# Earlier weights for the last two down-projection units, wider modulation columns, and low parts last in two first blocks

## The chip, the cores and the metric

The kernel runs on one core of one Trainium2 chip. The metric is the device time in microseconds (us) of one execution; three executions of the kernel before gave 900.03 to 900.54 us.

## The reference

One batch of 256 tokens of width 1024 passes two transformer blocks in float32. What matters here is the end of the first and the start of the second:

```python
# first block, end
h = rms_norm(x, ln_ffn_pre)
f = (silu(h @ w_ffn_gate) * (h @ w_ffn_up)) @ w_ffn_down     # hidden width 2816
x = x + rms_norm(f, ln_ffn_post)
# second block, start
mod = silu(c) @ w_ada + b_ada                                # six rows of 1024
sh1, sc1, g1, sh2, sc2, g2 = split(mod, 6)
u = rmsnorm(h, norm_mix_g) * (1 + sc1) + sh1
z = u @ w_in                                                 # 4296 columns
```

Before these stand the two attentions and the mixing of the first block, after them the retention, the sparse attention, and 16 experts of which each token takes two.

## The kernel before, in words

**Products in three.** Every float32 operand of a large product is split in a high part, which ScalarE writes (line 302), and a low part, raw less high, which VectorE writes (line 304). A product is then three matmuls per 128 rows of k (`mm3`, lines 320 to 322): high by high, activation high by weight low, activation low by weight high. Tokens stand in two chunks of 128, c = 0 and c = 1. The activation is the stationary operand, the weight the moving one.

**Weights.** `stream` requests a piece of weights on SP's queue into one of three raw buffers; `unit` splits it into one of four `hi` and four `lo` buffers, or, for `units_ahead`, into tiles of the large pool, so that a block's weights can lie split before its activation exists. A raw buffer is free again when its low parts are written. SP's queue is in order: a request that waits for a raw buffer holds those behind it.

**Order.** A scheduler places the instructions of each engine by their order in the program and by what is ready in its own model. `after(ins)` puts an instruction behind another one of the same engine. In the `with tc.manual_schedule` block near the end of `build` TensorE's order is the program's.

**The first join** is at the start of the first block's feed-forward: `post_norm` of chunk 0, `raw_T` (transposes, high parts by ScalarE on line 401, low parts by VectorE on line 404), then the gate's first 512 columns from units split ahead (`ready`), with chunk 1's norm and transposes between the two chunks' products.

**The second join** is between the blocks. The down-projection runs by units of 256 hidden rows (`out_step`, 11 units, numbers 0 to 10), the last two in one step: all of chunk 0 first, then, behind `mod_row(2)`, all of chunk 1. Its sums stand in three `s` banks and one `o` bank of PSUM. For a chunk then come `post_norm` (squares on ScalarE, line 247; a multiply by the gain, line 415; a row of one-column operations for the root, lines 255 to 265 and 422, 423; the update of x, line 428), `row_rstd` (squares and root again), `modulated_T` (two multiplies, line 379; eight transposes, line 361; eight high parts, line 385; eight low parts, line 388) and its products with two blocks of `w_in_2` split ahead, 512 columns (`ready`) and 200 columns (`ready2`). The table `ENGS` says for each norm and chunk whether the root's one-column operations are on VectorE (V) or GpSimd (G). `mod_cols` turns a row of the modulation into columns by eight products with ones (line 589), each of which TensorE takes in two passes; it stands twice, for rows 3 and 4, behind chunk 0's products.

Of the kernel before, what the change touches and what calls it, by code (L numbers as in the profile page):

```python
# [13 lines left out]
ALU = mybir.AluOpType  # L14
# [3 lines left out]
D = 1024  # L18
FF = 2816
EPS = 1e-6  # L20
AHEAD = (1, 2)
ENGS = ("VG", "VV", "VV", "VG", "VV")
ORDER = "0ab1cqkdgKgQ"
RSQRT_MAGIC = 1597463007.0 - 2.0 ** 22 - 2.0 ** 31
GN_EPS = 1e-5
# [88 lines left out]
def build(tc, A, out, dbg=None):  # L114
# [12 lines left out]
    with es:  # L127
# [47 lines left out]
        def P(which, shape):  # L175
            return {"s": ps_s, "o": ps_o, "b": ps_b}[which].tile(shape, F32, tag=which, name=which)
# [63 lines left out]
        def col(name, j=0, n=1):  # L240
            return colp[:, COL[name] + j:COL[name] + j + n]
# [43 lines left out]
        def stream(shape, srcs):  # L285
            raw = rawp.tile(shape, F32, tag="raw", name="raw")
            for dst, src in srcs(raw):
                nc.sync.dma_start(dst, src)
            return raw

        def unit(raw, ahead=False):

            kc, n = raw.shape[1], raw.shape[2]
            if ahead:
                hi, lo = B([128, kc, n], F32R), B([128, kc, n], F32R)
            else:
# [10 lines left out]
        def units_ahead(w, n0, n, src=None):  # L307

            us = []
            m = 2 if n > 256 else 4  # L310
            for k0 in (0, 4):
                raw = stream([128, 4, n], src(k0) if src else lambda r: [(r, wslice(w, k0, 4, n0, n))])
                us += [unit(raw[:, k:k + m, :], True) for k in range(0, 4, m)]
            return [(k, [b[:, k % m, :] for b in us[k // m]]) for k in range(8)]

        def wslice(w, k0, kc, n0, n):
            return w[k0 * 128:(k0 + kc) * 128, n0:n0 + n].rearrange("(c p) n -> p c n", p=128)

        def mm3(o, a, b, start, stop):
            PE.matmul(o, a[0], b[0], start=start, stop=False)  # L320
            PE.matmul(o, a[0], b[1], start=False, stop=False)  # L321
            return PE.matmul(o, a[1], b[0], start=False, stop=stop)  # L322

        def tok_block(act, w, n0, n, kc=8, src=None, between=None, piece=4, first=None, ready=None):

            acc = [P("b", [128, n]) for _ in range(2)]
            parts = []
            if ready is not None:
                parts = [ready]
            for k0 in range(0, kc if ready is None else 0, 4):  # L330
                m = min(4, kc - k0)
                raw = first if first is not None and not k0 else stream([128, m, n], src(k0) if src else lambda r: [
                    (r[:, i:i + piece], wslice(w, k0 + i, min(piece, m), n0, n)) for i in range(0, m, piece)])
                for k1 in range(0, m, 2):
                    ks = range(k1, min(k1 + 2, m))
                    u = unit(raw[:, k1:ks.stop, :])
                    parts.append([(k0 + k, [b[:, k - k1, :] for b in u]) for k in ks])
            if between and first is None and ready is None:
                parts = [sum(parts, [])]
            for part in parts:  # L340
                for c in range(2):
                    if between and c and part is parts[0]:
                        between(last)
                    for k, b in part:
                        last = mm3(acc[c], [a[k][:, c * 128:(c + 1) * 128] for a in act], b, k == 0, k == kc - 1)
            return acc
# [193 lines left out]
        def modc(i):  # L540
            return modT[:, i, :]
# [40 lines left out]
        def mod_cols(v, pt=None):  # L582

            m = mod_m[v]
            own = pt is None
            if own:
                pt = P("b", [128, 8, 32])
            for k in range(8):
                PE.matmul(pt[:, k, :], m[:, k * 128:(k + 1) * 128], one1[:, 0:32], start=True, stop=True)
            if own:  # L590
                V.tensor_tensor(modT[:, v, :], pt[:, :, 0], col("b_ada_2", v * 8, 8), op=ALU.add)

        ada_gen = ada_steps()

# [311 lines left out]
        def out_acc():  # L906
            return [[P("s", [128, 512]), P("s", [128, 512])], [P("s", [128, 512]), P("o", [128, 512])]]

        def out_step(acc, acts, w, j, nk, between=None):

            us = []
            for i in range(len(acts)):
                raw = stream([128, 2, D], lambda r: [(r, wslice(w, 2 * (j + i), 2, 0, D))])
                us.append([unit(raw[:, :, h * 512:(h + 1) * 512]) for h in range(2)])
# [62 lines left out]
        modvars = {}  # L977

        def block2_shift(pm):
            V.tensor_tensor(modT[:, 3:5, :], pm[:, :, :, 0], col("b_ada_2", 24, 16).rearrange("p (a b) -> p a b", a=2),  # L980
                            op=ALU.add)

        def block2_mods():
            pm = P("b", [128, 2, 32])
# [82 lines left out]
        for b in range(1, 6):  # L1067
            acts += turned_acts(ts)
            n = 512 if b < 5 else 256
            ts = hidden_rows(tok_block(hT, w_fg, b * 512, n), b * 512, n)  # L1070
            out_step(oacc, acts[2 * b - 2:2 * b - 1], w_fd, 2 * b - 2, 22)
            if b == 2:
                gain1 = load_row(A["norm_mix_g_2"])
            if b < 5:
                out_step(oacc, acts[2 * b - 1:2 * b], w_fd, 2 * b - 1, 22)
                ada(9)
            else:
                block2_rel()
            if b == 3:
                first_mods()  # L1080
        acts += turned_acts(ts)
        w_in2 = A["w_in_2"][0]
        ready = units_ahead(w_in2, 0, 512)

        ready2 = units_ahead(None, 0, 200, lambda k0: lambda r: [
            (r[:, :, 0:128], wslice(w_in2, k0, 4, 3584, 128)), (r[:, :, 128:200], wslice(w_in2, k0, 4, 4224, 72))])

        dtv = modvars["dtv"]
        cos2 = lambda c: K(f"cos{c}")
# [5 lines left out]
        turns = []  # L1095
        g1s = []

        def products(acc, units, c):
            for k, b in units:
                i = mm3(acc[c], [a[k][:, c * 128:(c + 1) * 128] for a in uT], b, k == 0, k == 7)  # L1100
            return i

        with tc.manual_schedule(engines={mybir.EngineType.PE}):
            out_step(oacc, acts[9:], w_fd, 9, 22, lambda: g1s.append(mod_row(2)))
            post_norm(oacc, post, 0, 2, rfc[0])
            *marks, xni = modulated_T(*uT, 0, row_rstd(0, 4), gain1, modc(0), (), "s")
            accs = [[P("b", [128, n]) for _ in range(2)] for n in (512, 200)]
            products(accs[0], ready, 0)
            products(accs[1], ready2, 0)
            pm = P("s", [128, 2, 8, 32])  # L1110
            mod_cols(3, pm[:, 0])
            mod_cols(4, pm[:, 1])
            post_norm(oacc, post, 1, 2, rfc[1], (), (xni,))
# [606 lines left out]
```

## Time and profile before

| | us |
|---|---|
| median of three runs | 900.38 |
| the profiled execution itself | 899.23 |
| its span, first to last instruction | 897.4 |
| TensorE busy in it | 864.0 (96%) |
| VectorE busy | 646.0 (72%) |
| ScalarE busy | 407.0 (45%) |
| GpSimd busy | 6.3 (1%) |
| mean granted TensorE clock | 0.988 |

Times below are microseconds from the start of the span. The ends of matmuls are modelled, so in a row of matmuls the distance from start to start is read, not the duration. The clock is a share of full speed: 1.00 is 2.4 GHz, 0.50 is 1.2 GHz.

### The profile page before, as it was taken

Reading aid. Unit: us, or ns where it says so; the run is one execution under the profiler, and the core shown is the slowest. Engines: PE = TensorE matmul, PEld = TensorE weight load, DVE = VectorE, ACT = ScalarE, POOL = GpSimd, SP = SyncE. Lnnn points to the kernel's source line nnn. Section 1 sums busy time; section 2 is a strip of 40 time slices with the busy share of each in tenths; the row PEclk is TensorE's granted clock in tenths of the full one; section 3 lists DMA queues with packets and bytes.
Section 4 is the critical chain, followed back from the end, with each engine's and each line's share of the span. In section 5 each row is a group of like instructions: output and inputs, shape, how many; then the busy total and the mean of one; then the engine's idle time right before and its main releaser. Section 6 shows DMA issues by size and latency. Waiting matters only on the chain.

```text
span 897.4 us, 13319 instructions
## 1 busy us (share of the span) xinstructions
PE 864.0 (96%) x4854; PEld 681.4 (76%) x4854; DVE 646.0 (72%) x1579; ACT 407.0 (45%) x737; POOL 6.3 (1%) x20
## 2 busy tenths in 40 slices
PE   8999999999999999999998999999999999999994
PEld 7777877888777788888895788889889987535541
DVE  6788787647986998888876796798865587333424
ACT  6554665556554644443454334433365354211212
POOL 0100000000000000000000000000000001000000
PEclk9999999999999999999998899999999999999998
DMA  8644452528787488988767045556547778699981
GB/s 304 199 159 129 128 166 68 174 83 296 272 298 270 139 285 289 333 313 283 282 204 253 1 141 150 179 159 194 158 133 259 228 252 308 195 384 333 359 324 50
DMA packets 104589, 195.94 MB, mean 218 GB/s; under 512 B 9892, under 2 KB 43547, under 8 KB 104518
## 3 DMA queue, kind: packets, MB, share of 16 engines
q1 hardware_dynamic: 103816, 194.12, 63.4%
q8 instruction: 40, 0.66, 0.3%
q10 hardware_dynamic: 702, 0.91, 0.3%
q14 instruction: 31, 0.25, 0.1%
HBM read 193.94 MB, written 1.06 MB: 217 GB/s over the span
## 4 chain that ended last, share of the span: by engine, by line
PE 76%; DVE 12%; ACT 5%; DMA 3%; issue 2%; POOL 1%; SPq 0%; ACTq 0%; DVEq 0%; POOLq 0%
PE b L322 14%; PE b L321 14%; PE b L320 14%; PE b L1537 6%; DVE lo L304 3%; PE b L1556 3%; PE s L361 3%; PE s L320 3%; PE s L322 3%; PE s L321 3%; ACT hi L302 2%; PE s L462 2%; PE b L1479 2%; PE s L1574 1%; DMA raw<-in_w_in 1%
## 5 line engine op out<-in xcount | busy, mean ns | idle before, releaser
L304 DVE TENSOR_TENSOR lo<-raw,hi 128x512 fp32r<-128x512 f32 (+4 forms) x447 | 270.7, 638 | 89.1 <-ACT hi L302 88.2
L302 ACT ACTIVATE hi<-raw 128x1024 fp32r<-128x1024 f32 (+4 forms) x220 | 218.2, 999 | 232.3 <-PE b L322 103.1
L320 PE MATMUL b<-hi,big 128*128 128x512 f32 (+3 forms) x502 | 190.8, 380 | 1.8 <-ACT hi L302 0.7
L321 PE MATMUL b<-lo,big 128*128 128x512 f32 (+3 forms) x502 | 190.4, 380 | 0.2 <-DVE lo L304 0.2
L322 PE MATMUL b<-hi,big 128*128 128x512 f32 (+3 forms) x502 | 189.7, 378 | 0.0
L321 PE MATMUL b<-big,hi 128*128 128x256 f32 x392 | 112.6, 287 | 0.0
L320 PE MATMUL b<-big,hi 128*128 128x256 f32 x392 | 112.5, 287 | 0.0
L322 PE MATMUL b<-big,lo 128*128 128x256 f32 x392 | 111.3, 284 | 0.0
L320 PEld LDWEIGHTS b<-hi,big 128*128 128x128 f32 x502 | 94.6, 188 | 19.9 <-ACT hi L302 1.5
L321 PEld LDWEIGHTS b<-lo,big 128*128 128x128 f32 x502 | 94.5, 188 | 17.3 <-issue 1.3
L322 PEld LDWEIGHTS b<-hi,big 128*128 128x128 f32 x502 | 94.5, 188 | 17.0 <-issue 0.5
L320 PEld LDWEIGHTS b<-big,hi 128*128 128x128 f32 x392 | 75.2, 192 | 2.2 <-issue 1.7
L321 PEld LDWEIGHTS b<-big,hi 128*128 128x128 f32 x392 | 75.0, 191 | 1.4 <-issue 1.2
L322 PEld LDWEIGHTS b<-big,lo 128*128 128x128 f32 x392 | 75.0, 191 | 0.5 <-issue 0.3
L1537 PE MATMUL b<-big 128*64 128x512 f32 x128 | 57.8, 596 | 0.0
L561 DVE SCALAR_TENSOR_TENSOR big<-big,csil 128x1024 f32<-128x1024 f32 x40 | 51.1, 1278 | 1.2 <-DMA big<-in_w_ada 1.1
L320 PE MATMUL s<-hi,act 128*128 128x512 f32 x66 | 27.1, 410 | 4.5 <-ACT hi L302 4.5
L1556 PE MATMUL b<-big,pT 128*64 128x512 f32 x128 | 28.9, 593 | 1.1 <-DVE pT L1546 1.1
L1537 PE MATMUL b<-raw,big 128*64 128x512 f32 x64 | 28.8, 593 | 0.0
L321 PE MATMUL s<-lo,act 128*128 128x512 f32 x66 | 26.6, 403 | 0.0
L322 PE MATMUL s<-hi,act 128*128 128x512 f32 x66 | 26.4, 400 | 0.0
L1491 ACT ACTIVATE pT<-b 128x256 f32<-128x256 f32 x8 | 3.1, 385 | 49.2 <-PE b L1537 49.2
(373 smaller groups left out, 1316.5 us busy)
## 6 DMA issues: line engine op xcount, KB each, us to landing
raw<-in_w_in SPq DMA_DIRECT2D x34, 1024.0 KB, 5.3
big<-in_w_ada SPq DMA_DIRECT2D x48, 512.0 KB, 6.6
big<-in_w_exp_down SPq DMA_DIRECT2D x32, 512.0 KB, 6.7
raw<-in_w_ffn_down SPq DMA_DIRECT2D x11, 1024.0 KB, 5.0
raw<-in_w_ffn_gate SPq DMA_DIRECT2D x10, 1024.0 KB, 8.0
raw<-in_w_ffn_up SPq DMA_DIRECT2D x10, 1024.0 KB, 5.1
raw<-in_w_o SPq DMA_DIRECT2D x8, 1024.0 KB, 5.7
raw<-in_w_gate SPq DMA_DIRECT2D x8, 1024.0 KB, 5.3
```

The costliest lines, as they stand in the source:

```text
L302: S.activation(hi, raw, AF.Copy)
L304: V.tensor_tensor(lo[:, a:a + m], raw[:, a:a + m], hi[:, a:a + m].bitcast(F32), op=ALU.subtract)
L320: PE.matmul(o, a[0], b[0], start=start, stop=False)
L321: PE.matmul(o, a[0], b[1], start=False, stop=False)
L322: return PE.matmul(o, a[1], b[0], start=False, stop=stop)
L361: turned[:] = [PE.transpose(dst[:, i, :], s, ident)]
L462: PE.matmul(scs[i][:, a:b], q[:, c * 128:(c + 1) * 128], k[:, 0:b - a], start=fresh[i], stop=False)
L561: V.scalar_tensor_tensor(m, wt, csil[:, k:k + 1], m, op0=ALU.mult, op1=ALU.add)
L1479: PE.matmul(pt[:, k, :], xs(c, (2 * k2 + k) * 128, 128), hot[:, c, :], start=(i == 0), stop=(i == 3))
L1537: PE.matmul(pu[i * 64:(i + 1) * 64, :].rearrange("p (a n) -> p a n", a=2), xg[k // 4][:, k % 4, s0:s0 + 64], win[2 * p + i][k], start=(k = ...
L1556: PE.matmul(py[i * 64:(i + 1) * 64, :], hT2[:, k, i * 64:(i + 1) * 64], wdn[2 * p + i][k][:, hs], start=(k == 0), stop=(k == 1))
L1574: PE.matmul(yacc[c][h], hT.bitcast(F32) if one else hT, y, start=False, stop=(p == 7 and (i == 1 or one)))
```

## The change

- The last two down-projection units (9 and 10) are requested and split before the first block of `w_in_2`, where they stood behind it, and behind both halves of the 200-column block.
- The 200-column block is requested in two halves (k 0 to 3 and k 4 to 7). The second is requested behind chunk 1's multiplies in the program, and its low parts are put behind them on VectorE. Chunk 0 is multiplied with the first half early, with the second one late.
- `mod_cols` moves 128 columns of ones in place of 32, at a distance of 16, so that each overwrites most of what the one before wrote and its first column stays. Row 3 comes right behind the down-projection, ahead of chunk 0's transposes; row 4 between chunk 0's two blocks. Their bank is of the `b` pool in place of `s`.
- Both first blocks issue all products of the high activations of a chunk first, then those of the low ones (`chunk_products`).
- In the norm behind the feed-forward (index 2 of `ENGS`) chunk 1's one-column operations go to GpSimd, and its multiplies (line 415) come behind the last low part of chunk 0, where they came behind its line 379.

```diff
-ENGS = ("VG", "VV", "VV", "VG", "VV")
+ENGS = ("VG", "VV", "VG", "VG", "VV")
...
+        def chunk_products(o, act, units, c, start=True, stop=True):
+
+            hi, lo = [[a[k][:, c * 128:(c + 1) * 128] for k, _ in units] for a in act]
+            for i, (k, b) in enumerate(units):
+                PE.matmul(o, hi[i], b[0], start=start and i == 0, stop=False)
+                PE.matmul(o, hi[i], b[1], start=False, stop=False)
+            for i, (k, b) in enumerate(units):
+                last = PE.matmul(o, lo[i], b[0], start=False, stop=stop and i == len(units) - 1)
+            return last
...
# tok_block
+                    if part is ready:
+                        last = chunk_products(acc[c], act, part, c)
+                        continue
...
# mod_cols
-                pt = P("b", [128, 8, 32])
+                pt = P("b", [128, 512])
...
-                PE.matmul(pt[:, k, :], m[:, k * 128:(k + 1) * 128], one1[:, 0:32], start=True, stop=True)
+                PE.matmul(pt[:, k * 16:k * 16 + 128], m[:, k * 128:(k + 1) * 128], one1, start=True, stop=True)
...
-        def out_step(acc, acts, w, j, nk, between=None):
+        def out_units(w, j):
+            raw = stream([128, 2, D], lambda r: [(r, wslice(w, 2 * j, 2, 0, D))])
+            return [unit(raw[:, :, h * 512:(h + 1) * 512]) for h in range(2)]
+
+        def out_step(acc, acts, w, j, nk, between=None, us=None):
...
+        outs = [out_units(w_fd, j) for j in (9, 10)]
         acts += turned_acts(ts)
         w_in2 = A["w_in_2"][0]
         ready = units_ahead(w_in2, 0, 512)
...
+        ready2 = [units_ahead(None, 0, 200, shared, (0,))]
...
         with tc.manual_schedule(engines={mybir.EngineType.PE}):
-            out_step(oacc, acts[9:], w_fd, 9, 22, lambda: g1s.append(mod_row(2)))
+            out_step(oacc, acts[9:], w_fd, 9, 22, lambda: g1s.append(mod_row(2)), outs)
             post_norm(oacc, post, 0, 2, rfc[0])
-            *marks, xni = modulated_T(*uT, 0, row_rstd(0, 4), gain1, modc(0), (), "s")
+            pm = P("b", [128, 2, 256])
+            mod_cols(3, pm[:, 0])
+            _, low, xni = modulated_T(*uT, 0, row_rstd(0, 4), gain1, modc(0), (), "s")
             accs = [[P("b", [128, n]) for _ in range(2)] for n in (512, 200)]
-            products(accs[0], ready, 0)
-            products(accs[1], ready2, 0)
-            pm = P("s", [128, 2, 8, 32])
-            mod_cols(3, pm[:, 0])
+            chunk_products(accs[0][0], uT, ready, 0)
             mod_cols(4, pm[:, 1])
-            post_norm(oacc, post, 1, 2, rfc[1], (), (xni,))
+            chunk_products(accs[1][0], uT, ready2[0], 0, True, False)
+            post_norm(oacc, post, 1, 2, rfc[1], (), (low,))
             *marks, xni = modulated_T(*uT, 1, row_rstd(1, 4), gain1, modc(0), (), "s")
-            products(accs[0], ready, 1)
-            products(accs[1], ready2, 1)
+            with after(xni):
+                ready2.append(units_ahead(None, 0, 200, shared, (4,)))
+            chunk_products(accs[0][1], uT, ready, 1)
+            chunk_products(accs[1][0], uT, ready2[1], 0, False, True)
+            chunk_products(accs[1][1], uT, ready2[0] + ready2[1], 1)
             with after(*marks):
                 block2_shift(pm)
```

## Rows read from the trace of the kernel before

**Rows 1.** Engine totals of the page: busy us, share of the span, instructions.
```profile
PE 864.0 (96%) x4854; PEld 681.4 (76%) x4854; DVE 646.0 (72%) x1579; ACT 407.0 (45%) x737; POOL 6.3 (1%) x20
```
**Rows 2.** TensorE's waits: who waited for whom, us in total, times, longest.
```profile
PE s L320 <- ACT hi L302: 4.5, 1, 4.5
PE s L361 <- DVE t2d L379: 2.1, 1, 2.1
...
PE b L322 <- DVE big L404: 1.3, 2, 0.9
```
**Rows 3.** Stretches of the second join: length, busy us (count) by engine, clock, DMA.
```profile
474.30:478.70 4.40, 0.00 (x0) 0.00 (x0) 1.82 (x5) 1.69 (x5) 0.00 (x0) 0.74 0.96 384
478.70:483.40 4.70, 4.65 (x11) 3.40 (x12) 4.47 (x8) 2.95 (x4) 0.00 (x0) 0.52 0.95 328
...
496.00:500.30 4.30, 4.23 (x15) 3.13 (x16) 4.21 (x13) 2.18 (x8) 0.00 (x0) 0.60 0.01 2
510.50:513.90 3.40, 3.40 (x14) 2.66 (x14) 1.08 (x5) 2.25 (x9) 0.00 (x0) 0.51 0.00 0
```
**Rows 4.** TensorE's timeline of the second join: start, duration, instruction, [idle before].
```profile
478.75 0.80 PE L320 MATMUL s<-hi,act 128*128 128x512 f32 x1 [4.48 <-ACT hi L302]
...
485.23 0.39 PE L320 MATMUL s<-hi,act 128*128 128x512 f32 x1
...
486.59 1.88 PE L574 MATMUL b<-big,one 128*128 128x512 f32 x4
...
496.06 1.66 PE L361 MATMUL s<-ident,t2d 128*128 128x128 f32 x8 [2.10 <-DVE t2d L379]
497.37 0.78 PE L320 MATMUL b<-big 128*128 128x512 f32 x1
...
504.36 0.25 PE L320 MATMUL b<-big 128*128 128x200 f32 x1
...
507.02 3.69 PE L589 MATMUL s<-one,big 128*128 128x32 f32 x32
510.52 1.94 PE L361 MATMUL s<-ident,t2d 128*128 128x128 f32 x8
...
521.34 0.60 PE L361 MATMUL s<-ident,t2d 128*128 128x128 f32 x4
```
**Rows 5.** SP's queue in the second join: start and duration of two requests.
```profile
460.23 0.37 SPq L288 DMA_DIRECT2D raw<-in_w_in  x1
...
472.53 0.37 SPq L288 DMA_DIRECT2D raw<-in_w_ffn_down  x1
```
**Rows 6.** ScalarE's timeline of the second join.
```profile
474.30 0.64 ACT L1051 ACTIVATE act<-b 128x256 fp32r<-128x256 f32 x2
477.64 2.00 ACT L302 ACTIVATE hi<-raw 128x1024 fp32r<-128x1024 f32 x2 [2.71 <-DMA raw<-in_w_ffn_down]
```
**Rows 7.** VectorE's timeline of the second join.
```profile
496.58 0.68 DVE L415 TENSOR_TENSOR t<-s,big 128x512 f32<-128x512 f32 x1
...
497.93 2.16 DVE L388 SCALAR_TENSOR_TENSOR big<-s,modT,big 128x128 fp32r<-128x128 f32 x8
...
502.61 1.42 DVE L428 SCALAR_TENSOR_TENSOR x<-t,sm1d,x 128x512 f32<-128x512 f32 x2
...
507.15 1.41 DVE L379 SCALAR_TENSOR_TENSOR t2d<-x,sm1d,big 128x512 f32<-128x512 f32 x2
```
**Rows 8.** GpSimd's timeline of a root's eight operations: first, sixth and last.
```profile
750.65 0.30 POOL L255 TENSOR_SCALAR sm1d<-sm2d 128x1 f32<-128x1 f32 x1 [722.71 <-ACT junk L247]
...
752.61 0.96 POOL L265 TENSOR_SCALAR sm1d<-sm1d 128x1 f32<-128x1 f32 x1
...
754.12 0.29 POOL L265 TENSOR_SCALAR sm1d<-sm1d 128x1 f32<-128x1 f32 x1
```
**Rows 9.** TensorE's timeline elsewhere: one product with 128 moving float32 columns, then the next.
```profile
580.25 0.39 PE L1245 MATMUL o<-big,pT 128*128 128x128 f32 x2
580.47 0.39 PE L1246 MATMUL o<-big,pT 128*128 128x128 f32 x2
```

More of the change, by code (lines that the diff above doesn't have):

```diff
@@ L305, in unit, with units_ahead @@
             return hi, lo
-        def units_ahead(w, n0, n, src=None):
-            us = []
+        def units_ahead(w, n0, n, src=None, k0s=(0, 4)):
+            parts = []
             m = 2 if n > 256 else 4
-            for k0 in (0, 4):
+            for k0 in k0s:
                 raw = stream([128, 4, n], src(k0) if src else lambda r: [(r, wslice(w, k0, 4, n0, n))])
-                us += [unit(raw[:, k:k + m, :], True) for k in range(0, 4, m)]
-            return [(k, [b[:, k % m, :] for b in us[k // m]]) for k in range(8)]
+                us = [unit(raw[:, k:k + m, :], True) for k in range(0, 4, m)]
+                parts += [(k0 + k, [b[:, k % m, :] for b in us[k // m]]) for k in range(4)]
+            return parts
         def wslice(w, k0, kc, n0, n):
@@ L586, in mod_cols @@
             if own:
-                pt = P("b", [128, 8, 32])
+                pt = P("b", [128, 512])
             for k in range(8):
-                PE.matmul(pt[:, k, :], m[:, k * 128:(k + 1) * 128], one1[:, 0:32], start=True, stop=True)
+                PE.matmul(pt[:, k * 16:k * 16 + 128], m[:, k * 128:(k + 1) * 128], one1, start=True, stop=True)
             if own:
-                V.tensor_tensor(modT[:, v, :], pt[:, :, 0], col("b_ada_2", v * 8, 8), op=ALU.add)
+                V.tensor_tensor(modT[:, v, :], pt[:, 0:128].rearrange("p (k n) -> p k n", k=8)[:, :, 0],
+                                col("b_ada_2", v * 8, 8), op=ALU.add)
         ada_gen = ada_steps()
@@ L907, in out_acc @@
             return [[P("s", [128, 512]), P("s", [128, 512])], [P("s", [128, 512]), P("o", [128, 512])]]
-        def out_step(acc, acts, w, j, nk, between=None):
[L911 to L914, printed above, removed]
+        def out_units(w, j):
+            raw = stream([128, 2, D], lambda r: [(r, wslice(w, 2 * j, 2, 0, D))])
+            return [unit(raw[:, :, h * 512:(h + 1) * 512]) for h in range(2)]
+        def out_step(acc, acts, w, j, nk, between=None, us=None):
+            us = us or [out_units(w, j + i) for i in range(len(acts))]
             n = range(len(acts))
@@ L979, in block2_shift @@
         def block2_shift(pm):
-            V.tensor_tensor(modT[:, 3:5, :], pm[:, :, :, 0], col("b_ada_2", 24, 16).rearrange("p (a b) -> p a b", a=2),
-                            op=ALU.add)
+            V.tensor_tensor(modT[:, 3:5, :], pm[:, :, 0:128].rearrange("p a (k n) -> p a k n", k=8)[:, :, :, 0],
+                            col("b_ada_2", 24, 16).rearrange("p (a b) -> p a b", a=2), op=ALU.add)
         def block2_mods():
@@ L1083, in build @@
         ready = units_ahead(w_in2, 0, 512)
-        ready2 = units_ahead(None, 0, 200, lambda k0: lambda r: [
-            (r[:, :, 0:128], wslice(w_in2, k0, 4, 3584, 128)), (r[:, :, 128:200], wslice(w_in2, k0, 4, 4224, 72))])
+        shared = lambda k0: lambda r: [
+            (r[:, :, 0:128], wslice(w_in2, k0, 4, 3584, 128)), (r[:, :, 128:200], wslice(w_in2, k0, 4, 4224, 72))]
+        ready2 = [units_ahead(None, 0, 200, shared, (0,))]
         dtv = modvars["dtv"]
@@ L1096, in build @@
         g1s = []
[L1098 to L1101, printed above, removed]
         with tc.manual_schedule(engines={mybir.EngineType.PE}):
-            out_step(oacc, acts[9:], w_fd, 9, 22, lambda: g1s.append(mod_row(2)))
+            out_step(oacc, acts[9:], w_fd, 9, 22, lambda: g1s.append(mod_row(2)), outs)
             post_norm(oacc, post, 0, 2, rfc[0])
-            *marks, xni = modulated_T(*uT, 0, row_rstd(0, 4), gain1, modc(0), (), "s")
+            pm = P("b", [128, 2, 256])
+            mod_cols(3, pm[:, 0])
+            _, low, xni = modulated_T(*uT, 0, row_rstd(0, 4), gain1, modc(0), (), "s")
             accs = [[P("b", [128, n]) for _ in range(2)] for n in (512, 200)]
-            products(accs[0], ready, 0)
-            products(accs[1], ready2, 0)
-            pm = P("s", [128, 2, 8, 32])
-            mod_cols(3, pm[:, 0])
+            chunk_products(accs[0][0], uT, ready, 0)
             mod_cols(4, pm[:, 1])
-            post_norm(oacc, post, 1, 2, rfc[1], (), (xni,))
+            chunk_products(accs[1][0], uT, ready2[0], 0, True, False)
+            post_norm(oacc, post, 1, 2, rfc[1], (), (low,))
             *marks, xni = modulated_T(*uT, 1, row_rstd(1, 4), gain1, modc(0), (), "s")
-            products(accs[0], ready, 1)
-            products(accs[1], ready2, 1)
+            with after(xni):
[3 more added lines that the diff above has]
+            chunk_products(accs[1][1], uT, ready2[0] + ready2[1], 1)
             with after(*marks):
```

## The prediction

> **What bounds the kernel now.** I read the page's totals first: TensorE is busy 96% of the span [rows 1], so time is to be had where it stands still or runs at half clock; the change takes no product away. Next come TensorE's waits [rows 2]: the longest is 4.5 us, for a high part of line 302 at an `s` bank; the others that the change touches are 2.1 us for line 379 and, twice, 1.3 us together, for the low parts of line 404. The first two lie in the second join, the last in the first. Third, the second join by stretches [rows 3]: the granted clock is 0.52 for 4.7 us behind the long wait, 0.60 for 4.3 us behind the 2.1 us one, and 0.51 for 3.4 us behind the 32 short modulation products, where TensorE had not stopped. So a long pause is paid twice, and a run of 32-column products costs clock without a pause. Last, the timelines, for the places. TensorE stops at 478.75 − 4.48 = 474.27, resumes at 478.75 with the last two down-projection units, transposes chunk 0 from T0 = 496.06 and chunk 1 from T1 = 510.52, and leaves the join at 521.34 [rows 4]. The units are late because SP asks for the first only at 472.53, behind the requests for `w_in_2`, the first of them at 460.23 [rows 5]; its high parts start when it has landed, at 477.64 [rows 6].
>
> **The change part by part.** At full clock a 512-column matmul takes (486.59 − 485.23) / 6 = 0.227 us [rows 4]; 24 take 5.45. All is summed against the profiled execution, 899.23 us (span 897.4); the median, 900.38, lies 1.15 above it and is taken to move by as much.
>
> *First join, high activations first: −1.3.* Both waits come where the first low activation is used [rows 2]. With 16 matmuls (3.6 us) ahead of the first low product, the eight low parts, 2.16 us on VectorE for that shape [rows 7], are in time. Nothing is added. Ends: 0, if the high parts on ScalarE are the next wait, and −1.9, if the restart gains too. I take the row.
>
> *Last two units first, the pause: −3.4.* SP can ask at 460.23 and a few us later for what it asks at 472.53 [rows 5]; with 5.1 us from request to use (477.64 − 472.53, [rows 5, 6]) both units are there before 470. Their splits need `hi` and `lo` buffers that unit 8 holds, and it is done before TensorE stops at 474.27; the last of the four is used only 2.7 us behind the start. What is late next are the activations: high parts at 474.30 to 474.94 [rows 6], low parts by about 475.3. So the start is 475.3 for 478.75. Ends: 474.7 (−4.1) and 477.5 (−1.2), if ScalarE and VectorE have splits of `w_in_2` queued ahead of the activations.
>
> *The clock behind it: −2.4.* Chunk 0's 24 matmuls take 486.59 − 478.75 = 7.84 us [rows 4] at 0.52 [rows 3], against 5.45. A pause of 1 us remains. Ends: 0 and −2.4; I take all of it, the gate is a rival below.
>
> *What is pushed back: +0.8.* The 512-column block and half of the 200-column one are now split behind the units: on VectorE eight low parts of 0.6 us and one of 0.5. From about 475.7 it needs 5.3 us, to 481.0, while chunk 0's first multiply wants it near 480.2. Ends: 0, and +2.0 if one of these requests lands late, for VectorE's queue is in order and the norm stands behind. The other half of the 200 columns holds its raw buffer until chunk 1's multiplies; behind it in SP's queue stand the next block's weights, which TensorE wants 10.8 us behind T1, so there is cover for twice the 5.1 us.
>
> *T0 to T1: −3.8.* From chunk 0's last sum to T0, 496.06 − 486.59 = 9.5 us [rows 4], the path is ScalarE and VectorE alone, and stays. TensorE, idle for 2.1 us ahead of T0 [rows 2], now has row 3's modulation there, 16 matmuls of (510.52 − 507.02) / 32 = 0.11 us, 1.75 us [rows 4]. With 128 moving columns I price them the same: two of that shape elsewhere start 0.22 us behind the two before [rows 9]; ends 0.11 and the 0.227 of 512 columns (+1.9 for each row, the first of them hidden).
>
> From T0 to T1 it was 14.46 us: 1.3 to the first product, 504.36 − 497.37 = 7.0 for 24 large matmuls (1.5 too long, at clock 0.60 [rows 3]), 2.66 for 24 of 200 columns, 3.5 for 32 of modulation [rows 4]. Now TensorE has 1.2 + 5.45 + 1.75 + 1.33 = 9.75, the other half of the 200 columns comes later. Late next is VectorE. Chunk 0's low parts end at T0 + 4.0, and chunk 1's two multiplies, which stood ahead of them at T0 + 0.5 in a gap where VectorE waits for ScalarE, come behind them: 1.3 us more, to T0 + 5.3 [rows 7]. In return the one-column operations, on VectorE up to 502.61, go to GpSimd, whose queue is empty but for 20 instructions in all [rows 1]. There eight take 754.41 − 750.65 = 3.8 us [rows 8], so ten 4.7. They can begin between the end of the products (T0 − 2.1) and T0 + 0.5, where VectorE read the same banks [rows 2, 7]; I take the middle, T0 − 0.8, and they end at T0 + 3.9, hidden. So x is updated from T0 + 5.3, before from 502.61, T0 + 6.55; the 4.54 us to line 379 [rows 7] and 0.8 to the transposes stay. T1 = T0 + 10.65, where TensorE waits 0.9 us; 14.46 − 10.65 = 3.8. Ends: −2.3, with half clock behind T0 again, and −4.7, if TensorE itself sets T1.
>
> Here a rule speaks against the change. The sixth of the eight operations took 0.96 us where the first took 0.30 and the last 0.29 [rows 8]. The Trainium skill, GPSIMD Engine Reference, section Specifications, says that GpSimd's interface to SBUF is shared with VectorE and contended when VectorE runs operations with two SBUF inputs, such as line 379. The trace agrees in so far as one of these short operations is long; by the rule all ten could be, which is the third rival.
>
> *T1 to the end of the join: −0.1.* 10.8 us before [rows 4], 3.4 of them at 0.51 [rows 3]; now 1.25 + 5.45 + 1.33 + 2.66 = 10.7: the moved 200-column work eats what the clock gives back. One wait is new: the `b` pool has four banks, so the last block takes the modulation's, free once VectorE has read it behind chunk 1's low parts. By chunk 0's spacing that is T1 + 4.3, and TensorE comes there at T1 + 8.0. Ends: −0.5 and +1.4 (half clock again).
>
> Behind the join the products are as before and I let the whole shift through.
>
> Sum: −1.3 − 3.4 − 2.4 + 0.8 − 3.8 − 0.1 = −10.2. The profiled execution goes from 899.2 to 889.0, the median to **890.2**.
>
> **The rivals.** *The splits stand in the way.* ScalarE and VectorE take pushed splits ahead of the activations (pause −1.2, the clock falls as now) and of the norm (+2.0): −1.3 − 1.2 + 2.0 − 3.8 − 0.1 = −4.4, **896**. For it: VectorE is at splits for 4.47 of the 4.7 us behind today's pause [rows 3]. Against: the activations stand ahead of the `w_in_2` splits in the program. Half of it gives 893.
>
> *The gate falls again.* Pauses of up to 1 us remain. With half clock once more behind T0 and T1, the two steps give −2.3 and +1.4: **893**. For it: 0.51 came without any pause [rows 3]. Against: that was behind 32-column products, and those go.
>
> *GpSimd is slow beside VectorE.* Ten operations of 0.96 with 0.1 between take 10.6 us, to T0 + 9.8; then x, and T1 = T0 + 15.1, 0.7 later than now; the −3.8 is gone: **895**. One long row in the three shown speaks for it, the seven short ones of the eight's 3.8 us against it.
>
> *Slower.* The clock falls in the pause near 474 and, with short pauses ahead of every group, is not given back until the join ends. At 0.52 a 512-column matmul takes 0.227 / 0.52 = 0.43 us, 0.2 more; the join has 96, 19 us, of which the two chains of norms hide about 5: 890 + 14 = **904**. It passes the time of before once about 75 of the 96, (10.2 + 5) / 0.2, are low. Against: behind each of today's pauses the low clock lasted under 5 us [rows 3].
>
> *It does not do what it says:* the scheduler puts the units' splits behind those of `w_in_2` again. Then only the first join, T0 to T1 and the last step gain: **895**.
>
> **How the numbers follow.** The forecast has 0.60, splits in the way and a schedule that undoes the order 0.17, the gate 0.10, GpSimd 0.05, slower 0.05, and 0.03 for mixtures that end near zero. The range is 886.8 to 895.5. Below stand the other ends of the steps, −1.9 − 4.1 − 2.4 − 4.7 − 0.5 = −13.6 with nothing pushed back; above, the rivals but for the first at its full price. A measurement of this kernel can tell about 0.2%, 1.8 us, from no change: faster 0.92, within it 0.03, slower 0.05.
>
> **What would show it.** No wait of 0.4 us at the third matmul of the feed-forward's first block. A pause under 1.5 us ahead of the last two units, and their first 24 matmuls in 5.5 us at clock 1.00. Modulation products at 0.11 us between the down-projection and T0. T1 − T0 near 10.7, with GpSimd's ten operations over before x is updated. No low clock from 474 to the end of the join. The prediction is wrong if the clock is under 0.7 in two of these stretches, if VectorE is at splits when the squares of chunk 0 are done, or if TensorE has a new wait in the 30 us behind the join.

## The result, and the profile after

The changed kernel takes 889.3 us in the median of four runs (888.7 to 890.68); beside it the kernel before took 900.2 (899.62 to 900.54). The ratio is 0.9877, 95% interval 0.9855 to 0.9899. The profiled execution took 890.68 us, span 888.9.

Totals of the page after, to be set against [rows 1]: busy us, share of the span, instructions.

```profile
PE 860.7 (97%) x4854; PEld 680.1 (77%) x4854; DVE 643.7 (72%) x1569; ACT 406.1 (46%) x737; POOL 9.9 (1%) x30
```

TensorE does the same 4854 matmuls in 3.3 us less busy time. Ten instructions have gone from VectorE to GpSimd. Helper lines have moved by some 14: line 361 of before is 375 now, 379 is 393, 388 is 402, 415 is 429, 428 is 442.

TensorE's waits after: who waited for whom, us in total, times, longest. Of the three in [rows 2], one is left.

```profile
PE s L375 <- DVE t2d L393: 2.4, 2, 1.9
```

The second join by stretches after: length, busy us (count) of TensorE, its weight loads, VectorE, ScalarE and GpSimd, then clock, DMA share and GB/s. In [rows 3] the same work had clocks of 0.52, 0.60 and 0.51.

```profile
474.30:475.64 1.34, 1.34 (x8) 0.48 (x7) 0.93 (x2) 1.34 (x3) 0.00 (x0) 1.00 1.04 405
475.64:481.20 5.56, 5.56 (x27) 4.59 (x25) 5.56 (x11) 4.05 (x7) 0.00 (x0) 1.00 0.43 116
...
492.29:496.79 4.50, 4.50 (x23) 3.63 (x24) 3.24 (x10) 2.93 (x9) 2.56 (x7) 1.00 0.00 2
...
502.70:513.40 10.70, 10.63 (x68) 9.39 (x69) 10.01 (x24) 5.96 (x12) 0.00 (x0) 1.00 0.32 100
```

TensorE's timeline after, for [rows 4]: the transposes of unit 10's activations, the first product of the last two units, chunk 0's last sum, the 16 matmuls of a modulation row (eight products of two passes), T0 and T1.

```profile
475.23 0.66 PE L375 MATMUL b<-ident,t 128*128 128x128 f32 x4
475.64 0.47 PE L321 MATMUL s<-hi,act 128*128 128x512 f32 x1
...
481.20 1.88 PE L588 MATMUL b<-big,one 128*128 128x512 f32 x4
...
488.41 1.95 PE L604 MATMUL b<-one,big 128*128 128x128 f32 x16
...
492.29 1.32 PE L375 MATMUL s<-ident,t2d 128*128 128x128 f32 x8 [1.93 <-DVE t2d L393]
...
502.76 1.32 PE L375 MATMUL s<-ident,t2d 128*128 128x128 f32 x8 [0.50 <-DVE t2d L393]
```

There is no pause ahead of the last units: 475.64 follows the transposes at once, where [rows 4] had 4.48 us of idle time.

**Where the time went.** Segments are read from start to start in TensorE's timeline: the first join from chunk 0's transposes to the next block; the second from unit 8's first product to units 9 and 10, to chunk 0's last sum, to T0, to T1, to the end.

| us | before | after | change | forecast |
|---|---|---|---|---|
| first join | 15.33 | 13.51 | −1.82 | −1.3 |
| unit 8 to units 9 and 10 | 11.64 | 6.93 | −4.71 | −3.4 |
| chunk 0's 24 products | 7.84 | 5.56 | −2.28 | −2.4 |
| last sum to T0 | 9.47 | 11.09 | +1.62 | +0.8 |
| T0 to T1 | 14.46 | 10.47 | −3.99 | −3.8 |
| T1 to the end | 10.82 | 10.71 | −0.11 | −0.1 |
| sum | | | −11.29 | −10.2 |

The spans differ by 8.5 us only, since the profiled execution after reached the first join 3.1 us later (at 293.35, before at 290.23), in code that is the same. Over all the profiled executions of this study that point lies between 289.5 and 296.5. So totals can't judge edits under 2 us. The steps inside the joins can: the first join came out between 13.46 and 13.51 in every trace with the new order of its products. The step from chunk 0's last sum to T0 is less steady: it took 10.77 to 11.26 in the six traces in which the half-block's split stands ahead of the norm (the whole change twice, low parts interleaved, 32 columns, root on VectorE, multiplies ahead). "From the first join on" below is the span less the start of chunk 0's transposes there: 607.2 before, 595.6 after, 11.6 less.

### The profile page after: what moved, and what is told of

It reads as the page before. It is cut to its first block, busy times and chain, and to the rows that moved or that the text cites. A ratio compares the mean times of both kernels' runs of the same rounds, so it can differ in the third digit from the quotient of the medians.

```text
span 888.9 us, 13325 instructions
## 1 busy us (share of the span) xinstructions
PE 860.7 (97%) x4854; PEld 680.1 (77%) x4854; DVE 643.7 (72%) x1569; ACT 406.1 (46%) x737; POOL 9.9 (1%) x30
## 3 DMA queue, kind: packets, MB, share of 16 engines
HBM read 193.94 MB, written 1.06 MB: 219 GB/s over the span
## 4 chain that ended last, share of the span: by engine, by line
PE 76%; DVE 12%; ACT 6%; DMA 3%; issue 2%; POOL 1%; ACTq 0%; SPq 0%; DVEq 0%; POOLq 0%
PE b L322 14%; PE b L321 14%; PE b L323 14%; PE b L1554 6%; DVE lo L304 3%; PE b L1573 3%; PE s L375 3%; ACT hi L302 3%; PE s L323 2%; PE s L321 2%; PE s L322 2%; PE s L476 2%; DMA raw<-in_w_in 2%; PE b L1496 2%; PE s L1591 1%
```

## The experiments

Medians are of 4 to 12 executions; the segments are those of one profiled execution each. The kernel before, beside them, had medians of 901.25 (first four kernels), 900.72 (next four) and 900.96 (last four). All segments in us:

| kernel | median | ratio, interval | first join | chunk 0's sum to T0 | wait at T0 | T0 to T1 | T1 to end | from first join on |
|---|---|---|---|---|---|---|---|---|
| before | 900.2 | | 15.33 | 9.47 | 2.10 | 14.46 | 10.82 | 607.2 |
| whole change | 889.3 | 0.9877 [0.9855, 0.9899] | 13.51 | 11.09 | 1.93 | 10.47 | 10.71 | 595.6 |
| units alone | 896.91 | 0.9959 [0.9944, 0.9974] | 15.33 | 12.49 | 5.12 | 14.95 | 10.54 | 603.0 |
| low parts interleaved | 889.42 | 0.9877 [0.9859, 0.9894] | 15.33 | 11.00 | 1.85 | 11.29 | 11.34 | 598.2 |
| 32 columns | 890.19 | 0.9891 [0.9872, 0.9909] | 13.51 | 11.11 | 2.04 | 11.19 | 10.65 | 596.3 |
| root on VectorE | 891.02 | 0.9897 [0.988, 0.9915] | 13.48 | 10.94 | 1.79 | 11.35 | 10.69 | 596.6 |
| whole change again | 889.02 | 0.9871 [0.9849, 0.9893] | 13.48 | 11.26 | 2.11 | 11.15 | 10.65 | 596.5 |
| split behind norm | 888.23 | 0.9856 [0.983, 0.9882] | 13.51 | 9.84 | 0.68 | 10.75 | 10.68 | 594.5 |
| multiplies ahead | 888.6 | 0.9858 [0.9833, 0.9883] | 13.46 | 10.77 | 1.62 | 9.81 | 10.64 | 594.5 |
| both edits | 886.24 | 0.984 [0.9815, 0.9864] | 13.50 | 9.98 | 0.83 | 9.80 | 10.63 | 593.8 |
| both, 32 columns | 888.07 | 0.9872 [0.9841, 0.9903] | 13.47 | 9.83 | 0.77 | 9.81 | 10.64 | 593.6 |
| both, rows together | 889.65 | 0.9879 [0.9857, 0.99] | 13.51 | 10.77 | none | 10.13 | 10.68 | 595.0 |
| both, rows together, 32 | 888.58 | 0.9869 [0.9846, 0.9891] | 13.47 | 10.69 | none | 9.55 | 10.69 | 594.0 |
| both, root on VectorE | 889.96 | 0.9885 [0.9859, 0.9911] | 13.46 | 10.05 | 0.90 | 11.87 | 10.70 | 595.7 |

**Units alone.** The kernel before, with one edit:

```diff
+        outs = [out_units(w_fd, j) for j in (9, 10)]
         acts += turned_acts(ts)
...
-            out_step(oacc, acts[9:], w_fd, 9, 22, lambda: g1s.append(mod_row(2)))
+            out_step(oacc, acts[9:], w_fd, 9, 22, lambda: g1s.append(mod_row(2)), outs)
```

> The kernel before with one part of the change: the last two down-projection units are requested and split ahead of the w_in_2 blocks. My account of the result: TensorE's pause ahead of these units goes (-4.7 us) and with it the half clock behind it (-2.3), while the splits pushed back make chunk 0's norm 1.5 to 2.5 us late; the rest of the second join stays as it was, its low clock behind T0 too. So 900.2 - 7.0 + 2.0 = 895.2, within 894.5 to 896. Rival A, the whole gain comes from this part and the others do nothing: 889 to 890. Rival B, the gain needs the parts together, since the late norm eats what the units give: 898 or more.

Units 9 and 10 started 6.92 us behind unit 8 and chunk 0's products took 5.56: the pause and the clock behind it belong to this edit, −7.0 us together. But the norm came 3.0 us later, since both halves of the 200-column block now stood ahead of it, and T0 to T1 grew by 0.49 with the clock at 0.54 behind a wait of 5.12 us. The join gained 3.8, the median 4.3. The pause and the clock have the size of the theory; the norm was later than the 1.5 to 2.5 us I gave it, and the median, 896.91, lies above my 894.5 to 896. What came on top was the second half-block: on VectorE its low part, 1.06 us behind a wait of 0.47 for ScalarE, stood among the root's operations, from 485.46 on.

**Low parts interleaved.** The whole change, three matmuls per 128 rows of k again:

```diff
             for i, (k, b) in enumerate(units):
                 PE.matmul(o, hi[i], b[0], start=start and i == 0, stop=False)
                 PE.matmul(o, hi[i], b[1], start=False, stop=False)
-            for i, (k, b) in enumerate(units):
```

> The whole change, but both first blocks issue three matmuls per k again, the low activation third. My account: the first join loses the 1.8 us that it gained; in the second TensorE waits about 0.7 us at the third matmul behind T0 and behind T1, of which 0.5 is hidden by its wait ahead of T1: +1.8 + 0.9 = +2.7, 892.0. Rival, the order matters only in the first join, by the two waits of before: +1.3, 890.6. A third way, no effect, since another wait takes the place: 889.3.

TensorE's timeline of the first join, this kernel: the third matmul of each chunk.

```profile
294.15 0.51 PE L331 MATMUL b<-big 128*128 128x512 f32 x1 [0.43 <-DVE big L417]
...
301.95 0.50 PE L331 MATMUL b<-big 128*128 128x512 f32 x1 [0.85 <-DVE big L417]
```

Both waits for the low parts in [rows 2] are back and the first join is 15.33 again: the whole −1.82 is this edit's. Behind T1 the same order is worth 0.63. The segments show it; the median does not: I expected 892.0, and it is 889.42, against 889.3.

**32 columns.** The whole change with `one1[:, 0:32]` and an output 32 wide in `mod_cols`.

> The whole change with 32 moving columns in the modulation products again. My account: the wait of 1.9 us ahead of T0 is as long as the 2.1 us of before, and the clock stayed full only because 16 wide products stand ahead of it; with 32 columns half clock is granted behind T0 and again behind the second 16, T1 comes about 1 us later and the products behind it take 1 more: 890.5 to 892, granted clock under 0.7 in the 4 us behind T0. Rival: the columns do nothing for the clock here, since the narrow products no longer stand 32 in a row: clock 1.00 throughout, 889.3 within 0.4.

The clock was 0.62 behind T0 and T0 to T1 0.72 us longer; behind the other 16 modulation matmuls it stayed at 1.00. I first took this as proof that the wide columns keep the clock; the control below took that back.

**Root on VectorE.** The whole change with the norm's one-column operations of chunk 1 on VectorE (`"VV"` for `"VG"` in `ENGS`).

> The whole change with the one-column operations of chunk 1's root on VectorE again. My account: some of the ten fit the 1.3 us in which VectorE waits for ScalarE's high parts, the others, 0.8 to 1.3 us, stand between the multiplies and the update of x, and T1 comes as much later: 890.1 to 890.6, T1 - T0 near 11.5 where the whole change has 10.5. Rival A, all of them hide: 889.3. Rival B, GpSimd and VectorE hold each other up at the shared interface, and VectorE alone is no slower or faster: 889.3 or less, with line 393 and the low parts shorter than beside GpSimd.

T0 to T1 grew by 0.88, as expected. But here too the clock was 0.62 behind T0, and TensorE had no wait ahead of T1: the 0.88 can be the clock's. VectorE's own path had grown too: its line 393 for chunk 1 began 10.54 us behind T0, against 9.67 in the whole change, and with 0.8 us to the transposes that alone comes to T1.

**Whole change again.** The unaltered changed kernel.

> The changed kernel itself, unaltered, as the measure for the three runs beside it. Its second join took 44.76 us from unit 8's first matmul to the end in the trace already read, the first join 13.51; I expect both again within 0.1 us, and a total near 889.5 us. If the joins come out the same while the totals of the profiled executions differ by 1 us or more, then that scatter lies outside the joins and a step of under 1 us is to be read from the segments of a join.

The first join came out the same; the second took 45.55 us, 0.8 more than in the first trace, where I expected 0.1 at most. TensorE's restart at T0 and the 4.5 us behind it, in this execution:

```profile
488.95 1.78 PE L375 MATMUL s<-ident,t2d 128*128 128x128 f32 x8 [2.11 <-DVE t2d L393]
```

```profile
488.95:493.45 4.50, 4.50 (x17) 3.73 (x18) 2.99 (x10) 2.93 (x9) 2.57 (x7) 0.62 0.01 2
```

The very kernel whose first trace held 1.00 behind T0 has 0.62 here, and T0 to T1 is 11.15. So the 32 columns (11.19) cost nothing against it, and the root on VectorE moved T1 by at most 0.2 at that clock. That is since TensorE at the low clock sets T1 in the control: VectorE's line 393 began 9.92 us behind T0 there, so the root on VectorE had made VectorE's path 0.62 longer. The same stretch (4.5 us from T0) with 32 columns, then with multiplies ahead:

```profile
490.89:495.39 4.50, 4.50 (x17) 3.68 (x18) 3.03 (x10) 2.93 (x9) 2.56 (x7) 0.62 0.00 2
```

```profile
493.28:497.78 4.50, 4.49 (x23) 3.63 (x24) 4.44 (x12) 2.93 (x9) 2.56 (x7) 1.00 0.01 2
```

**Split behind norm.** The early request stays, but the first half of the 200-column block is split behind chunk 0's second square on ScalarE and behind chunk 1's update of x on VectorE; the second half's split stands behind chunk 1's squares too:

```diff
-        ready2 = [units_ahead(None, 0, 200, shared, (0,))]
+        first_half = stream([128, 4, 200], shared(0))
...
-            post_norm(oacc, post, 1, 2, rfc[1], (), (low,))
+            updated = post_norm(oacc, post, 1, 2, rfc[1], (), (low,))
+            split_first_half(norm_squares, updated)
...
-            with after(xni):
+            with after(xni, squares[-1]):
```

> Whole change, but the first half of the 200-column block, still requested early, is split later: on ScalarE behind the second square of chunk 0's norm, on VectorE behind chunk 1's update of x; the second half's high part also behind chunk 1's squares. My theory (the late half-block stands in ScalarE's in-order queue ahead of the second square, and its low part in VectorE's ahead of the second multiply): from chunk 0's last sum to T0 goes from 11.09 to about 9.5 us, as in the kernel before; T0 to T1 stays near 10.5; the join about 43.1, the time about 1.6 us under the whole change, 887.7. Rival (the 1.6 us come from the 512-column block's low parts on VectorE, which stand ahead of the norm in either kernel): the step stays within 0.4 us of 11.09.

First ScalarE after (the whole change): the first square, the half-block's split, the second square. Then VectorE after: low parts of the 512-column block, the first multiply, the half-block's low parts, the second multiply, the root's first operation. Then ScalarE of this kernel, the two squares and the split, and its VectorE, both multiplies and the root's first operation.

```profile
480.04 0.60 ACT L247 ACTIVATE junk<-s 128x512 bf16<-128x512 f32 x1 [1.04 <-PE s L323]
...
481.92 0.87 ACT L302 ACTIVATE big<-raw 128x800 fp32r<-128x800 f32 x1 [1.19 <-DMA raw<-in_w_in]
482.70 0.58 ACT L247 ACTIVATE junk<-s 128x512 bf16<-128x512 f32 x1
```

```profile
478.39 3.68 DVE L304 TENSOR_TENSOR big<-raw,big 128x512 fp32r<-128x512 f32 x6
482.00 0.67 DVE L429 TENSOR_TENSOR t<-s,big 128x512 f32<-128x512 f32 x1
482.82 1.06 DVE L304 TENSOR_TENSOR big<-raw,big 128x400 fp32r<-128x400 f32 x2 [0.16 <-ACT big L302]
483.80 0.68 DVE L429 TENSOR_TENSOR t<-s,big 128x512 f32<-128x512 f32 x1
484.40 0.26 DVE L436 TENSOR_SCALAR sm1d<-sm2d,rf 128x1 f32<-128x1 f32 x1
```

```profile
478.91 0.60 ACT L249 ACTIVATE junk<-s 128x512 bf16<-128x512 f32 x1 [1.07 <-PE s L325]
...
480.33 0.60 ACT L249 ACTIVATE junk<-s 128x512 bf16<-128x512 f32 x1 [0.73 <-PE s L325]
...
492.61 0.93 ACT L304 ACTIVATE big<-raw 128x800 fp32r<-128x800 f32 x1
```

```profile
480.84 1.27 DVE L431 TENSOR_TENSOR t<-s,big 128x512 f32<-128x512 f32 x2
482.04 0.25 DVE L438 TENSOR_SCALAR sm1d<-sm2d,rf 128x1 f32<-128x1 f32 x1
```

In the whole change ScalarE's queue stands 1.19 us at a weight that has not landed, with the square behind it, 2.66 us after the first; without it the second square follows the first after 1.42 us and needs only the product. On VectorE the half-block's low parts, 1.06 us, stand between the two multiplies, and of that queue's time only 0.16 us was a wait for ScalarE. The norm gets 1.25 us back of 1.62 (1.42 against the whole change's second trace).

The edit moves both splits, and no run moved one alone. The rows tell how the two stand together. From chunk 0's last sum to the root's first operation it was 3.20 us in the whole change and is 1.97 here. VectorE's low parts ended last there: with the weight on time they would have begun 0.16 us sooner, and no more. In the trace of the next kernel, "multiplies ahead", they waited for nothing, though ScalarE stood 0.82 us, and this step still took 2.90. Without them, though, the second multiply would have waited for the late square: in the kernel before it starts 0.72 us behind that square's start (487.57 and 486.85), which would be 483.42 for 483.80. By this estimate either split alone keeps most of the cost, and both had to move.

The rival named the eight low parts of the 512-column block, and those were left where they were: the first multiply starts behind them here as well (480.84), and they are what is left of the delay, 0.37 us.

**Multiplies ahead.** Chunk 1's multiplies behind line 393 again:

```diff
-            post_norm(oacc, post, 1, 2, rfc[1], (), (low,))
+            post_norm(oacc, post, 1, 2, rfc[1], (), (xni,))
```

> Whole change, but chunk 1's two multiplies by the gain stand behind line 393 of chunk 0 again, ahead of its low parts, as in the kernel before; the root stays on GpSimd. My theory (VectorE sets T1 by 0.5 us, and the multiplies behind the low parts are on that path): T0 to T1 goes from 10.47 to 9.8 us, where TensorE itself sets it, its wait ahead of T1 is gone, and 0.5 to 0.7 us are won. Rival (the low parts come 1.3 us later for it and TensorE waits for them at the low products): T0 to T1 is 10.5 or more, with a wait for a low part of line 402 in its place.

TensorE at T1, this kernel:

```profile
503.09 1.04 PE L375 MATMUL s<-ident,t2d 128*128 128x128 f32 x8
```

No wait is left ahead of T1, and T0 to T1 is 9.81: now TensorE sets it. No low product waits; this part of the change cost 0.66.

**Both edits.** The two edits above in one kernel.

> Both of the two edits: the split of the first half behind the norm and the multiplies ahead of the low parts. If both theories hold and add up: last sum to T0 9.5 us, T0 to T1 9.8, the join 42.4 us against 44.76, the time about 2.3 us under the whole change, near 887. If the late split takes the place that the multiplies set free on VectorE, T0 to T1 stays near 10.5 and the time is that of the first edit alone.

They add up: 9.98 and 9.80; the second join is 42.9 us, against 44.76 and 45.55. From the first join on it takes 593.8, 1.8 and 2.8 less than the whole change's two traces. The median, 886.24, is the lowest of all; its interval overlaps that of the whole change, and the next kernel, with the same segments, has 888.07. So that it beats the whole change rests on the segments.

**Both, 32 columns.**

> The two edits together (split of the first half behind the norm, multiplies ahead of the low parts) and 32 moving columns in the modulation products in place of 128. Open since the control: the unaltered whole change itself had the low clock behind T0 in one trace (pause of 2.11 us) and not in the other (1.93 us), so the low clock with 32 columns (pause of 2.04 us) may have come from the pause and not from the columns. Here the pause is only about 0.8 us. Theory (the pause decides, 16 products of either width do nothing): clock 1.00 behind T0 and T1, T0 to T1 9.80, the join 42.9 us within 0.2. Rival (narrow products count towards the pause, 1.7 + 0.8 us): clock 0.5 to 0.8 behind T0, T0 to T1 10.5 or more.

TensorE at T0 and T1, this kernel:

```profile
489.13 1.32 PE L377 MATMUL s<-ident,t2d 128*128 128x128 f32 x8 [0.77 <-DVE t2d L395]
...
498.94 1.07 PE L377 MATMUL s<-ident,t2d 128*128 128x128 f32 x8
```

Segment by segment this equals the wide columns within 0.15 us, at clock 1.00.

**Rows together, with 128 and with 32 columns.** `mod_cols(4, pm[:, 1])` right behind `mod_cols(3, pm[:, 0])`, ahead of T0.

> The two edits together, and the modulation products of both rows, 3 and 4, in one run of 32 right ahead of chunk 0's transposes, 128 columns each. TensorE now fills the pause ahead of T0: 3.4 us of products for a gap of 2.5, so T0 comes about 0.9 us later without a wait, and T0 to T1 goes from 9.8 to about 9.5, where VectorE sets it; the join about 43.5. Theory (wide products count as work): clock 1.00 behind T0. Rival (any run of 32 such products drops the clock, as in the kernel before): 0.5 behind T0 for 3 us or more, T0 to T1 over 10.5.

> As the run with both rows in one run of 32 products ahead of T0, but 32 moving columns each, which is how the kernel before ran them ahead of T1 (clock 0.51 behind them without a pause). Theory (32 narrow products in a row drop the clock, 32 wide ones do not, so the width matters for a long run only): clock 0.5 to 0.6 for about 3.5 us behind T0, T0 to T1 at least 0.7 longer than with the wide ones. Rival (width does nothing): clock and times equal to those with the wide ones.

The narrow kernel's timeline, and the clock behind its 32 matmuls:

```profile
484.56 3.65 PE L606 MATMUL b<-one,big 128*128 128x32 f32 x32
488.04 1.07 PE L377 MATMUL s<-ident,t2d 128*128 128x128 f32 x8
```

```profile
488.04:492.54 4.50, 4.48 (x25) 3.66 (x25) 3.64 (x11) 2.94 (x9) 1.86 (x7) 1.00 0.00 0
```

My theory for the narrow ones fell: 32 narrow matmuls in a row left the clock at 1.00 here. With wide ones the clock was 1.00 as well, and T0 to T1 was 0.58 longer, but not for the time of the wide matmuls: the scheduler put chunk 1's update of x and its square ahead of chunk 0's last high parts, and TensorE waited 1.12 us for one of these. As a comparison of times this pair is inconclusive.

**Both, root on VectorE.**

> The two edits together, with chunk 1's one-column operations of the norm on VectorE in place of GpSimd. In the first run of this kind the clock was low behind T0 as well, so its 0.9 us could be the clock's or the root's. Here the pause ahead of T0 is about 0.8 us and the clock should stay at 1.00. Theory (ten operations of 0.25 us stand in VectorE's chain from T0 to T1, part of them in gaps where it waits for ScalarE): T0 to T1 10.6 to 11.8 against 9.80, with a wait of 0.8 to 2 us ahead of T1 for line 395. Rival (VectorE has gaps for all of them, the earlier 0.9 us were the clock): T0 to T1 within 0.2 of 9.80.

TensorE at T1, and VectorE ahead of it: the end of the low parts, the first one-column operation behind them, the update of x.

```profile
503.11 1.10 PE L377 MATMUL s<-ident,t2d 128*128 128x128 f32 x6 [1.91 <-DVE t2d L395]
```

```profile
493.11 2.16 DVE L404 SCALAR_TENSOR_TENSOR big<-s,modT,big 128x128 fp32r<-128x128 f32 x8
495.19 0.14 DVE L259 TENSOR_SCALAR sm1d<-sm1d 128x1 f32<-128x1 f32 x1
...
497.48 1.42 DVE L444 SCALAR_TENSOR_TENSOR x<-t,sm1d,x 128x512 f32<-128x512 f32 x2
```

At full clock T0 to T1 is 2.07 longer, a little past my 11.8. From 495.19 to 497.48, 2.3 us, nine operations stand between the low parts and x. This is GpSimd's share in the kernel with both edits, cleared of the clock. In the whole change's own order it is smaller: there seven of the ten operations stood ahead of the low parts, and VectorE's line 393 came 0.62 us later than in the control, 0.87 later than in the first trace.

## Why the prediction was right, and where its terms were off

The forecast of 890.2 for 889.3 came from the right places: all six terms lie within 1.4 us of what was measured. That the sum is so near is in part luck: the two largest misses, −1.3 and +0.8, pull against each other, and the profiled execution kept the full clock behind T0, where four of the five traces with a pause of about 2 us there and the new order did not.

*The pause, −3.4 for −4.71.* Mis-sized, past my end of −4.1. I let the start wait for the activations' high and low parts. But `acts[9:]` holds those of unit 9 as well, which stood ready; only unit 10 needs the fresh ones, and it comes 12 matmuls later. (The 2.7 us that the prediction gives as the first use of the last buffer are these 12; the last of the four is wanted 18 matmuls behind the start, 4.1 us.) ScalarE wrote the high parts from 476.48 on, behind splits, as my first rival had it, and that cost nothing. ScalarE after, a split of `w_in_2` and the activations:

```profile
475.53 1.05 ACT L302 ACTIVATE big<-raw 128x1024 fp32r<-128x1024 f32 x1
476.48 0.64 ACT L1068 ACTIVATE act<-b 128x256 fp32r<-128x256 f32 x2
```

*The clock behind it, −2.4 for −2.28.* Right. The 0.52 that stands beside the 7.84 us held for 4.7 of them; over all of them the clock was 0.71. The term was taken from the times and does not change.

*Pushed back, +0.8 for +1.62.* Mis-sized. The engine was the one I reckoned with, VectorE, but its low parts of the 512-column block ended at 482.07 where I had 481.0 for all of them, and the half-block had two low parts of 0.5 us, not one, which waited 0.16 us for ScalarE and stood between the two multiplies. It was near the end that I gave for one late request (+2.0). SP's queue after, three requests, the half-block's first:

```profile
477.87 2.43 SPq L288 DMA_DIRECT2D raw<-in_w_in  x3
```

The request left only 0.08 us behind the last low part of unit 10 (VectorE, to 477.79), whose raw buffer it takes by the program's order of three buffers: early in the program was not early on the queue. The weight landed after chunk 0's first square was done (481.92 against 480.73), and ScalarE's queue stood at it too. One of my own signs of failure, VectorE at splits when the squares are done, so did show, at the price of one term. Taking the half-block's split away on both engines gave 1.25 back; how the 1.25 divide is read from rows, not from a run. The units alone, with twice the half-blocks ahead, paid 3.02.

*First join, −1.3 for −1.82.* The waits were the place; the size comes from starts, not from the waits' own 1.3: between the second and third matmul lay 0.82 and 1.30 us where 0.227 is normal, 1.66 too many, and each restart took 0.11 more. My end of −1.9 had said so.

*T0 to T1, −3.8 for −3.99.* Right in the profiled execution, −3.3 in the control with its low clock. By its parts in the first: GpSimd's ten operations took 4.5 us (forecast 4.7) and ended before x was wanted, VectorE set T1 by 0.5 us (0.9).

GpSimd's timeline after, second to sixth operation, and VectorE's line 393 beside them:

```profile
491.49 0.19 POOL L257 TENSOR_SCALAR sm1d<-sm1d 128x1 f32<-128x1 f32 x1
491.76 0.52 POOL L259 TENSOR_SCALAR sm1d<-sm1d 128x1 int32<-128x1 int32 x1
492.38 0.72 POOL L264 TENSOR_SCALAR sm1d<-sm1d 128x1 f32<-128x1 f32 x1
493.21 0.29 POOL L265 TENSOR_SCALAR sm1d<-sm1d 128x1 f32<-128x1 f32 x1
493.60 0.34 POOL L264 TENSOR_SCALAR sm1d<-sm1d 128x1 f32<-128x1 f32 x1
```

```profile
491.48 1.42 DVE L393 SCALAR_TENSOR_TENSOR t2d<-x,sm1d,big 128x512 f32<-128x512 f32 x2
```

The 0.72 lies beside VectorE's line 393 (491.48 to 492.90), which reads two SBUF operands; the same operation takes 0.34 later. The 0.96 of [rows 8] lies beside such an operation too (VectorE's line 1469 there, 752.33 to 753.47). In the profile after this touched one or two of the ten operations, and the 895 of that rival needed all ten. The Trainium skill, GPSIMD Engine Reference, section Specifications, says that GpSimd shares its SBUF interfaces with VectorE and contends with VectorE's operations that have two SBUF inputs; the trace agrees, though no run took line 393 away from beside GpSimd's operations.

*The gate falls again* came true by half, in some executions. Behind T0 the clock fell in one trace of the change and not in the other, for 0.68 us. Of the pauses of 1.79 to 2.11 us in this study (the column "wait at T0", and the 1.91 at T1 above) five were followed by 0.60 to 0.62 and two by 1.00; of those from 0.50 to 1.62 us at the same places none was followed by a low clock. Two lengths, 1.79 that fell and 1.93 that did not, show that the length alone doesn't decide. The Trainium skill, TensorE: Matmul & The Clock Gate, Part 1, says that the gate does not run in step with the kernel, so that the same kernel spends more or less at low clock from run to run; the two traces of one kernel agree (1.00 and 0.62).

*One reading of the profile before was wrong:* that "a run of 32-column products costs clock without a pause" [rows 3]. Neither 16 nor 32 such matmuls did so ahead of T0 where the pause was under 1 us (the kernels with both edits). What made the 0.51 behind T1 of before (and 0.58 with the units alone) is open: in both, 24 matmuls of 200 columns stood ahead of the 32, and no run took these apart. So the gain behind T1 came with the new order, and the width of the columns had no share in it that a run shows.

*The range.* Its upper end, 895.5, leaves out two of the rivals, the 896 and the 904, not the first alone.

## What to carry to other kernels

A transfer asked for early in the program is not yet free: look at which buffer its request waits for, in which queues its split will stand, and what stands behind it there. Here the split held up a norm on two engines at once, by its own time on one and by a late weight on the other. Before an edit is credited with a clock that stayed up, run the unaltered kernel a second time; here that one control overturned two verdicts. Where executions scatter by several us, small steps are judged from start to start inside the stretch that was changed, and by more than one trace.

## What was not expected of the hardware

Behind the same code nearly the same pause, 1.93 and 2.11 us, left TensorE at 2.4 GHz in one execution and at 1.2 GHz for most of 4.5 us in another, which moved T1 by 0.68 us. At T0 and T1 no pause of 0.50 to 1.62 us was followed by the low clock; without any pause, T1 of the kernel before and of the units alone was. That gives the split behind the norm a second use: it brings T0 1.25 us nearer and shortens the pause ahead of it to 0.7 to 0.9 us (none with the rows together), and none of the six traces with that edit has the low clock there.
